# S5 parameter preparation: order of the buffer's memset, the rows, C's turn and the loads of B and C

## The chip, the cores and the metric

The kernel runs on one core of a Trainium2 chip. The metric is the device time of one execution in microseconds (us). The engines are TensorE (PE; its weight loads are PEld), VectorE (DVE), ScalarE (ACT), GpSimd (POOL) and SyncE (SP). SP and POOL issue the DMA transfers that matter here; each engine takes its instructions strictly in program order.

## What is computed

Two layers on a sequence of 256 tokens of 1024 channels, float32. Each layer is FFN, mixer, FFN; mixer 0 is an S5 state-space mixer, mixer 1 a gated MLP.

```
h = LN(alpha*h + 0.5*swiglu(h, w_in[i,0], w_out[i,0]))
h = LN(alpha*h + mixer(h))          # S5 in layer 0, gMLP in layer 1
h = LN(alpha*h + 0.5*swiglu(h, w_in[i,1], w_out[i,1]))
```

The S5 mixer needs parameters that are worked out from its inputs alone:

```
dt = exp(log_dt);  mag = exp(a_re*dt)
lam = mag * (cos(a_im*dt) + i*sin(a_im*dt))
coef = (lam - 1) / (a_re + i*a_im)
bbar = coef * b                     # 64 groups x 64 states x 16 channels
h_t = lam*h_(t-1) + bbar*u_t;  y = Re(c*h)
```

## The kernel before, in words

The order of the instructions is written out by hand. `Stream` (line 44) carries all weights: a block of 128x2048 is loaded by SP into one of 3 raw buffers, split into hi (a cast on ScalarE, line 88) and lo (a subtraction on VectorE, line 89), both in one of 5 split buffers, and used by three matmuls per product (lines 201 to 203 and 208 to 210). `Stream.tick` (line 130) is called after each group of matmuls: it finishes the pending lo's, issues loads, splits a block and then runs one background function. In the first FFN a chunk of 256 hidden columns has four ticks in `chunk_in` (line 373) and two in `step_out`; `start_in` (line 409) is the special first chunk, with three ticks, 0 to 2.

The background of the first FFN is the S5 parameter work of `prepare_s5` (line 620). It is a list of items (first tick, cost, function), lines 941 to 990. Its own `tick` (line 994) adds 1.5 to a credit at each tick, at most to 2.25, and runs items from the head of the list as long as the tick number has reached the item's first tick and the credit is positive or the item's cost is 0:

```
credit[0] = min(credit[0] + PREP_US, 1.5 * PREP_US)
while work and work[0][0] <= ticks[0] and (credit[0] > 0.0 or work[0][1] == 0):
    _, cost, f = work.pop(0)
    credit[0] -= cost
    f()
```

The items that matter:
- `loads` (line 665) is run at once: POOL loads a_re, a_im, log_dt, d and b_glu as rows. `turn_a` (line 674) turns them on TensorE and copies them out on ScalarE; `ws.early` calls it in `start_in`.
- `exp` (line 693) has three parts on VectorE; the first use gives dt, the second mag. `angle` (line 720) multiplies a by dt, reduces the angle and calls Sin on ScalarE. `lambdas`, `coefs`, `coef`, `lam_power` (lines 732 to 764) are small VectorE operations.
- `seed` (line 775) is eight small POOL operations; `base_table` (line 788) is six of them, `table` (line 806) makes the turn tables on VectorE from the base table, which ScalarE copies.
- `load_b(part)` (line 825) issues 8 POOL loads into bq; `copy_b` (line 834) copies them to other partitions on ScalarE.
- `spread` (line 767): POOL writes the factors out (cf<-fac, line 769) and loads them back in another order (fac<-cf, line 771, four loads).
- `clear_rows` (line 838) clears the rows' buffer s on POOL. `b_rows(j, part)` (line 842) multiplies B with the factors (prod) and adds into s on VectorE; `b_turn` (line 851) turns s into w on VectorE and SP writes it to DRAM (rows<-w).
- `c_load(j)` (line 894) issues 8 POOL loads of C into cz; `c_turn` (line 903) turns cz into cc on VectorE, changes a sign, and puts two `pad` copies (ScalarE) into `behind`, which is run at the next tick. `c_lam` and `b_bar` (lines 910, 890) use cc and b.

The large buffers (tag q: s5a, ch, fac, cz, cc, w, tb, b, cl) share a pool of 6; s, pq and k share one buffer (tag bet).

Of the kernel before, what the change touches and what calls it, by code (L numbers as in the profile page):

```python
# [41 lines left out]
class Stream:  # L42
# [41 lines left out]
    def split(self, pieces=1, eng=None):  # L84
        nc = self.nc
        if self.lazy:
            raw, hi, lo = self.next_block()
            nc.scalar.copy(hi, raw)  # L88
            self.unfinished.append(lambda: nc.vector.tensor_tensor(lo, raw, hi.bitcast(F32), op=ALU.subtract))  # L89
            return  # L90
        eng = eng or [nc.vector]
        raw, hi, lo = self.next_block()
        w = SUB // pieces
        for p in range(pieces):
            s = slice(p * w, (p + 1) * w)
            nc.scalar.copy(hi[:, s], raw[:, s])  # L96
            eng[p % len(eng)].tensor_tensor(lo[:, s], raw[:, s], hi[:, s].bitcast(F32), op=ALU.subtract)  # L97
# [57 lines left out]
def hybrid(ctx: ExitStack, tc: tile.TileContext, a: dict, out: bass.AP, subs=SUBS):  # L155
# [24 lines left out]
    ws = Stream(nc, raw_p, split_p)  # L180

    def transpose_split(src, hi, lo, n, perm=False):


        ps = mm_p.tile([P, 512], F32, tag="mm", name="tps")
        for j in range(n):
            nc.tensor.transpose(ps[:, j * P:(j + 1) * P], src[:, j * P:(j + 1) * P], ident)
        v = ps[:, :n * P].rearrange("p (n t) -> p n t", n=n)
        if perm:
            v = v.rearrange("p n (k t) -> p n t k", t=T)  # L190
            hi, lo = (x.rearrange("p n (t k) -> p n t k", t=T) for x in (hi, lo))
        nc.scalar.copy(hi, v)
        nc.vector.tensor_tensor(lo, v, hi.bitcast(F32), op=ALU.subtract)

    def make_xt(t, perm=False, parts=range(2)):
        for g in parts:
            s = slice(4 * g, 4 * g + 4)
            transpose_split(h[t][:, 512 * g:512 * g + 512], xth[t][:, s], xtl[t][:, s], 4, perm)
# [64 lines left out]
    def in_mm(ids, t, ps, ks):  # L263
        for k in ks:
            wh, wl = ws.get(ids[k // 4])
            s = slice(512 * (k % 4), 512 * (k % 4) + 512)
            mm3(ps, xth[t][:, k], xtl[t][:, k], wh[:, s], wl[:, s], k == 0, k == KD - 1)

    def done(ids):
        for i in ids:  # L270
            ws.done(i)
# [61 lines left out]
    def ffn(ids, li, si, first, last):  # L333
# [20 lines left out]
        def in_act(c, t, ps):  # L354
            sgg = g_p.tile([P, 2, FC], F32, tag="sgg", name="sgg")
            sg, g = sgg[:, 0], sgg[:, 1]
            nc.scalar.activation(sg, ps[:, :FC], AF.Silu)
            nc.vector.tensor_tensor(g, ps[:, FC:], sg, op=ALU.mult)
            pend.append((c, t, g))
# [49 lines left out]
        def start_in():  # L409

            ps = [mm_p.tile([P, 512], F32, tag="mm", name="ips") for _ in range(2)]
            mm = lambda t, k: in_mm(ids["in"][0], t, ps[t], [k])
            make_xt(0, parts=[0])
            split = ws.split_pieces(4)
            split(0)
            make_xt(0, parts=[1])
            mm(0, 0)
            split(1)
            make_xt(1)
            mm(0, 1)  # L420
            for k in range(2):
                mm(1, k)
            for k in range(2, 4):
                split(k)
                for t in range(2):
                    mm(t, k)
            ws.early()
            split = ws.split_pieces(4)
            for k in range(4):
                split(k)  # L430
                for t in range(2):
                    mm(t, 4 + k)
                if k >= 2:
                    ws.tick(0)
            ws.fill()
            ws.tick(2)
            for t in range(2):
                in_act(0, t, ps[t])
            done(ids["in"][0])
# [180 lines left out]
    def prepare_s5(sm, qp, dram):  # L620
# [9 lines left out]
        V, G, A = nc.vector, nc.gpsimd, nc.scalar  # L630
        MUL, ADD, SUB, MAX, MIN = ALU.mult, ALU.add, ALU.subtract, ALU.max, ALU.min
# [4 lines left out]
        twice = lambda x: x.unsqueeze(1).broadcast_to([x.shape[0], 2, *x.shape[1:]])  # L636

        def tt(o, x, y, op, e=V):
            e.tensor_tensor(o, x, y, op=op)  # L639
            return o  # L640

        def ts(o, x, s1, op0, s2=None, op1=None, e=V):
            if op1 is None:
                s2, op1 = 1.0, MUL
            e.tensor_scalar(o, x, s1, s2, op0=op0, op1=op1)
            return o
# [6 lines left out]
        val = {}  # L653
# [39 lines left out]
        def exp(x, name):  # L693

            v, k, r, e = small("ex"), small("ek"), small("er"), both("ee")
            o = val[name] = small(name)

            def reduce():
                ts(v, x(), -170.0, MAX, 170.0, MIN)
                ts(k, v, 1.0 / math.log(2.0), MUL, ROUND, ADD)  # L700
                ts(k, k, -ROUND, ADD)
                stt(r, k, -LN2[0], MUL, v, ADD)
                stt(r, k, -LN2[1], MUL, r, ADD)

            def polynomial():
                ts(o, r, 1.0 / 5040.0, MUL)
                for n in (720.0, 120.0, 24.0, 6.0, 2.0, 1.0):
                    stt(o, o, 1.0 / n, ADD, r, MUL)

            def scale():  # L710
                ts(e[:, 0], k, -126.0, MAX, 127.0, MIN)
                tt(e[:, 1], k, e[:, 0], SUB)
                ts(e, e, 127.0, ADD, ROUND, ADD)
                V.tensor_scalar(e.bitcast(I32), e.bitcast(I32), 23, None, op0=ALU.logical_shift_left)
                stt(o, o, 1.0, ADD, e[:, 0], MUL)
                tt(o, o, e[:, 1], MUL)

            return (1.0, reduce), (1.5, polynomial), (1.2, scale)

        def angle():  # L720
            tt(val["ad"], val["aa"], twice(val["dt"]), MUL)
            th, n = val["ad"][:, 1], small("n")
            ts(n, th, 1.0 / (2.0 * math.pi), MUL, ROUND, ADD)
            ts(n, n, -ROUND, ADD)
            for part in TWO_PI:
                stt(th, n, -part, MUL, th, ADD)
            ts(th, th, 3.1415925, MIN, -3.1415925, MAX)
            z = val["zs"][0]
            A.activation(z[:, 0], th, AF.Sin, scale=0.5)
            A.activation(z[:, 1], th, AF.Sin)  # L730
# [143 lines left out]
        def pad(dst, src):  # L874
            for g in range(2):
                s = slice(64 * g, 64 * g + 64)
                A.copy(dst[s, :, g], src[s])

        behind = []
# [23 lines left out]
        def c_turn():  # L903
            cc = val["cc"] = big("cc", [P, 2, PAIRS, 16])
            V.transpose(cc.rearrange("p j q c -> p (j q c)"), val["cz"].rearrange("p j r c -> p (j r c)"))
            ts(cc[:, 1], cc[:, 1], -1.0, MUL)
            for j in range(2):
                behind.append(lambda j=j: pad(val["c", 0, j], cc[:, j]))

        def c_lam(d, j):  # L910
            if d > 1:
# [26 lines left out]
        def add(first, cost, f, *args):  # L938
            work.append((first, cost, lambda: f(*args)))
# [2 lines left out]
        ws.early = turn_a  # L942
        for cost, f in exp(lambda: val["ldt"], "dt"):
            add(1, cost, f)
        add(2, 1.4, angle)
        for part in range(2):
            add(2, 0, load_b, part)
        for cost, f in exp(lambda: val["ad"][:, 0], "mag"):
            add(3, cost, f)
        for part in range(2, 4):  # L950
            add(3, 0, load_b, part)
        add(4, 2.1, lambdas)
        add(4, 0, seed, 0)
        add(5, 1.4, coefs)
# [2 lines left out]
        add(5, 0, spread)  # L957
        for i in range(1, 7):
            add(5, 0, seed, i)
        add(5, 0, clear_rows)  # L960
        for d in (2, 3):
            add(5, 0.9, lam_power, d)
            for n in (32, 64):
                add(5, 0, copy_b, d - 2, n)
        late = [(base_table, level) for level in range(4)]
        for part in range(4):
            for j in range(2):
                add(10, 1.9, b_rows, j, part)
                if part < 2:
                    add(10, 0, copy_b, part + 2, (32, 64)[j])  # L970
                add(10, 1.3, b_turn, j, part)
                if late:
                    add(10, 0, *late.pop(0))
# [4 lines left out]
        for r in range(4):  # L978
            for level in (4, 5):
                add(20, (1.1, 1.9)[level - 4], table, r, level)  # L980
            if r == 1:
                add(20, 0, c_load, 0)
                add(20, 0, c_load, 1)
                add(20, 0, b_load)
        add(20, 0, pads, 2)
        add(30, 1.3, c_turn)
        for f, *args in [(c_lam, 1, 0), (b_bar, 0), (b_bar, 1), (c_lam, 1, 1)] + [(c_lam, d, j) for d in (2, 3) for j in range(2)]:
            add(30, 2.1, f, *args)
        add(50, 0, k_products, 0)
# [320 lines left out]
```

## Time and profile before

| | |
|---|---|
| median of 3 runs | 1002.95 us (1002.23 to 1005.33) |
| the profiled execution | 1001.06 us, span 999.2 us |
| TensorE busy | 955.0 us (96%) |
| VectorE busy | 648.1 us (65%) |
| ScalarE busy | 427.3 us (43%) |
| GpSimd busy | 158.9 us (16%) |

Matmuls are pipelined and their ends are modelled, so a busy TensorE is not TensorE at its peak. A row of a timeline has start, length, engine, line, operation, output<-input, shape and count; what stands in brackets at its end is the idle time of the engine just before and what ended it. POOL's loads appear there as issues, not as transfers. In a table of windows each engine has its busy time and its number of instructions, and the granted clock of TensorE is a share of 2.4 GHz.

### The profile page before, as it was taken

How to read it: one execution, taken by the hardware profiler on the slowest of the kernel's cores; microseconds unless marked ns; L12 is line 12 of the kernel's file. 1: busy time of each engine (PE TensorE's matmuls, PEld its weight loads, DVE VectorE, ACT ScalarE, POOL GpSimd, SP SyncE). 2: the span in 40 equal slices, each digit the busy share in tenths (PEclk: the TensorE clock that was granted, in tenths of full speed). 3: DMA queues.
4: the chain of work that ended last, by engine and by line, in shares of the span. 5: the costliest groups of instructions: out<-in, count | busy, mean ns of one | idle time of the engine just before them, and what ended most of it. 6: DMA issues, size and time to landing. Idle time of an engine off the chain costs nothing.

```text
span 999.2 us, 16604 instructions
## 1 busy us (share of the span) xinstructions
PE 955.0 (96%) x6988; PEld 866.1 (87%) x6988; DVE 648.1 (65%) x804; ACT 427.3 (43%) x507; POOL 158.9 (16%) x248
## 2 busy tenths in 40 slices
PE   6897999999998999999999999999999999999996
PEld 5896898987887779999998899999979879999995
DVE  4756999866897766454549654454698867363544
ACT  4562346633433344434343453434245355343530
POOL 7259152000565010000002000000011010000001
PEclk9898999999999999999999999999999999999999
DMA  9653897884565358464645867464537556646421
GB/s 251 195 177 127 262 292 232 257 320 172 206 233 176 121 182 269 140 224 156 214 166 167 276 214 240 136 228 152 211 127 264 158 169 222 200 168 212 152 102 42
DMA packets 132202, 195.10 MB, mean 195 GB/s; under 512 B 6992, under 2 KB 103808, under 8 KB 132128
## 3 DMA queue, kind: packets, MB, share of 16 engines
q1 hardware_dynamic: 127280, 182.34, 55.1%
q0 software_dynamic: 4560, 11.19, 3.7%
q8 instruction: 54, 0.88, 0.4%
q10 hardware_dynamic: 288, 0.52, 0.1%
q14 instruction: 20, 0.16, 0.0%
HBM read 184.07 MB, written 9.96 MB: 194 GB/s over the span
## 4 chain that ended last, share of the span: by engine, by line
PE 62%; DVE 19%; POOL 6%; issue 5%; DMA 4%; ACT 3%; SPq 0%; POOLq 0%; DVEq 0%; ACTq 0%
PE ips L210 10%; PE ips L209 10%; PE ips L208 10%; PE acc L201 7%; PE acc L202 7%; PE acc L203 7%; DVE lo L89 4%; DVE lo L97 3%; POOL rot L1081 3%; DVE rot L1087 1%; DVE pq L639 1%; DMA raw<-in_ffn_w_out 1%; PE ips L203 1%; DMA tc<-tb 1%; ACT hi L96 1%
## 5 line engine op out<-in xcount | busy, mean ns | idle before, releaser
L210 PE MATMUL ips<-xt,lo 128*128 128x256 f32 x1184 | 338.5, 286 | 13.2 <-DVE lo L89 10.5
L208 PE MATMUL ips<-xt,hi 128*128 128x256 f32 x1184 | 337.7, 285 | 0.0
L209 PE MATMUL ips<-xt,hi 128*128 128x256 f32 x1184 | 337.2, 285 | 0.0
L89 DVE TENSOR_TENSOR lo<-raw,hi 128x2048 fp32r<-128x2048 f32 x107 | 242.9, 2290 | 11.3 <-ACT hi L88 11.2
L210 PEld LDWEIGHTS ips<-xt,lo 128*128 128x128 f32 x1184 | 229.4, 194 | 14.9 <-DVE lo L89 11.9
L208 PEld LDWEIGHTS ips<-xt,hi 128*128 128x128 f32 x1184 | 229.7, 194 | 1.5
L209 PEld LDWEIGHTS ips<-xt,hi 128*128 128x128 f32 x1184 | 229.4, 194 | 1.4
L88 ACT CAST hi<-raw 128x2048 fp32r<-128x2048 f32 x107 | 204.0, 1909 | 48.1 <-PE acc L203 26.5
L201 PE MATMUL acc<-hi,gt 128*128 128x512 f32 x352 | 138.0, 392 | 1.0 <-ACT gt L406 1.0
L202 PE MATMUL acc<-lo,gt 128*128 128x512 f32 x352 | 137.7, 391 | 1.3 <-DVE lo L89 1.3
L398 DVE TENSOR_TENSOR sgg<-ips,sgg 128x256 f32<-128x256 f32 x74 | 31.1, 421 | 163.5 <-ACT sgg L397 163.3
L203 PE MATMUL acc<-hi,gt 128*128 128x512 f32 x352 | 137.1, 389 | 0.0
L397 ACT ACTIVATE sgg<-ips 128x256 f32<-128x256 f32 x74 | 28.4, 383 | 214.3 <-PE ips L210 214.1
L221 POOL TENSOR_SCALAR rstd<-mv 128x1 f32<-128x1 f32 x14 | 10.4, 741 | 635.6 <-DVE mv L247 611.9
L97 DVE TENSOR_TENSOR lo<-raw,hi 128x2048 fp32r<-128x2048 f32 (+1 forms) x54 | 89.7, 1694 | 22.8 <-ACT hi L96 22.8
L201 PEld LDWEIGHTS acc<-hi,gt 128*128 128x128 f32 x352 | 66.2, 188 | 14.4 <-ACT gt L406 1.8
L202 PEld LDWEIGHTS acc<-lo,gt 128*128 128x128 f32 x352 | 66.3, 188 | 14.1 <-DVE lo L89 1.9
L203 PEld LDWEIGHTS acc<-hi,gt 128*128 128x128 f32 x352 | 66.1, 188 | 14.2 <-DVE gt L407 0.3
L96 ACT CAST hi<-raw 128x2048 fp32r<-128x2048 f32 (+1 forms) x54 | 74.5, 1434 | 3.8 <-DMA raw<-in_ffn_w_in 3.1
L407 DVE TENSOR_TENSOR gt<-sgg,gt 128x256 fp32r<-128x256 f32 x74 | 31.6, 427 | 59.9 <-ACT gt L406 59.9
L406 ACT CAST gt<-sgg 128x256 fp32r<-128x256 f32 x74 | 30.0, 406 | 71.8 <-DVE sgg L398 71.7
L201 PE MATMUL ips<-hi,xt 128*128 128x512 f32 x112 | 45.3, 405 | 4.9 <-ACT hi L106 2.7
(231 smaller groups left out, 1224.9 us busy)
## 6 DMA issues: line engine op xcount, KB each, us to landing
raw<-in_ffn_w_in SPq DMA_DIRECT2D x172, 512.0 KB, 5.6
raw<-in_ffn_w_out SPq DMA_DIRECT2D x44, 1024.0 KB, 5.1
raw<-in_g_w_in SPq DMA_DIRECT2D x8, 1024.0 KB, 5.4
rows<-w SPq DMA_DIRECT2D x8, 512.0 KB, 6.1
raw<-in_s_w_in SPq DMA_DIRECT2D x4, 1024.0 KB, 7.3
raw<-in_s_w_glu SPq DMA_DIRECT2D x4, 1024.0 KB, 5.0
w<-rows SPq DMA_DIRECT2D x8, 512.0 KB, 6.4
tc<-tc SPq DMA_DIRECT2D x8, 512.0 KB, 5.8
```

What stands on the lines that cost most here:

```text
L88: nc.scalar.copy(hi, raw)
L89: self.unfinished.append(lambda: nc.vector.tensor_tensor(lo, raw, hi.bitcast(F32), op=ALU.subtract))
L96: nc.scalar.copy(hi[:, s], raw[:, s])
L97: eng[p % len(eng)].tensor_tensor(lo[:, s], raw[:, s], hi[:, s].bitcast(F32), op=ALU.subtract)
L201: nc.tensor.matmul(ps, xh, wh, start=start, stop=False)
L202: nc.tensor.matmul(ps, xh, wl, start=False, stop=False)
L203: nc.tensor.matmul(ps, xl, wh, start=False, stop=stop)
L208: nc.tensor.matmul(ps, wh, xh, start=start, stop=False)
L209: nc.tensor.matmul(ps, wh, xl, start=False, stop=False)
L210: nc.tensor.matmul(ps, wl, xh, start=False, stop=stop)
L398: nc.vector.tensor_tensor(g, ps[:, 1], sg, op=ALU.mult)
L407: nc.vector.tensor_tensor(x[:, 1], g, x[:, 0].bitcast(F32), op=ALU.subtract)
```

## The change

- `turn_a` is called earlier in `start_in`: after the second `make_xt`, ahead of three groups of three matmuls and two split pieces.
- The multiply of a by dt leaves `angle` (VectorE) and becomes `scaled` on POOL, put out as soon as dt is; `angle` costs 1.2 in the list and comes at tick 3.
- All 32 loads of B, `clear_rows` and all 16 loads of C follow `scaled` in POOL's queue. Before, B's loads had nothing to wait for, `clear_rows` followed the seeds and C's loads came with the tables.
- `c_turn` moves from the first tick 30 to 12, ahead of the rows; its two pad copies become an item of their own (`c_pads`) in its old place.
- The rows' first tick is 13 in place of 10.

```diff
@@ start_in
             make_xt(1)
+            ws.early()
             mm(0, 1)
...
-            ws.early()
             split = ws.split_pieces(4)
@@ prepare_s5
+        def scaled():
+            tt(val["ad"], val["aa"], twice(val["dt"]), MUL, G)
+
         def angle():
-            tt(val["ad"], val["aa"], twice(val["dt"]), MUL)
...
+        def c_pads():
             for j in range(2):
-                behind.append(lambda j=j: pad(val["c", 0, j], cc[:, j]))
+                pad(val["c", 0, j], val["cc"][:, j])
...
-        add(2, 1.4, angle)
-        for part in range(2):
+        add(2, 0, scaled)
+        for part in range(4):
             add(2, 0, load_b, part)
+        add(2, 0, clear_rows)
+        for j in range(2):
+            add(2, 0, c_load, j)
+        add(3, 1.2, angle)
         for cost, f in exp(lambda: val["ad"][:, 0], "mag"):
             add(3, cost, f)
-        for part in range(2, 4):
-            add(3, 0, load_b, part)
...
-        add(5, 0, clear_rows)
...
+        add(12, 1.6, c_turn)
         late = [(base_table, level) for level in range(4)]
         for part in range(4):
             for j in range(2):
-                add(10, 1.9, b_rows, j, part)
+                add(13, 1.9, b_rows, j, part)
...
             if r == 1:
-                add(20, 0, c_load, 0)
-                add(20, 0, c_load, 1)
                 add(20, 0, b_load)
         add(20, 0, pads, 2)
-        add(30, 1.3, c_turn)
+        add(30, 0, c_pads)
```

## Rows read from the trace of the kernel before

**Rows 1.** Busy time by engine in windows of 5 us, 75 to 90 us.

```profile
75.00:80.00 5.00, 3.65 (x18) 2.86 (x16) 0.00 (x0) 0.00 (x0) 3.92 (x16) 1.00 0.00 0
80.00:85.00 5.00, 0.00 (x0) 0.00 (x0) 2.89 (x3) 0.00 (x0) 4.65 (x10) 0.85 0.00 0
85.00:90.00 5.00, 4.34 (x18) 4.05 (x19) 4.99 (x5) 0.00 (x0) 4.84 (x8) 0.50 0.68 188
```

Columns: window and its length, then PE, PEld, DVE, ACT and POOL busy us (instructions), TensorE's granted clock, DMA share, GB/s.

**Rows 2.** The same table, one later window of 5 us and one of 25 us.

```profile
110.00:115.00 5.00, 5.00 (x44) 5.00 (x43) 4.93 (x10) 3.69 (x4) 0.00 (x0) 1.00 0.97 306
125.00:150.00 25.00, 24.93 (x186) 23.77 (x186) 24.72 (x47) 12.45 (x16) 14.86 (x20) 1.00 0.98 291
```

**Rows 3.** Timeline of VectorE, 29 to 195 us.

```profile
29.84 0.19 DVE L639 TENSOR_TENSOR dt<-dt,ee 128x32 f32<-128x32 f32 x1
...
50.43 2.34 DVE L89 TENSOR_TENSOR lo<-raw,hi 128x2048 fp32r<-128x2048 f32 x1
...
63.79 0.29 DVE L639 TENSOR_TENSOR ch<-p,q 128x32 f32<-128x32 f32 x2
69.85 1.39 DVE L639 TENSOR_TENSOR prod<-bq,fac 128x512 f32<-128x512 f32 x2 [5.77 <-DMA fac<-cf]
82.11 0.83 DVE L639 TENSOR_TENSOR s<-prod 128x256 f32<-128x256 f32 x2 [10.87 <-POOL s L840]
82.86 2.35 DVE L89 TENSOR_TENSOR lo<-raw,hi 128x2048 fp32r<-128x2048 f32 x1
...
86.29 2.24 DVE L89 TENSOR_TENSOR lo<-raw,hi 128x2048 fp32r<-128x2048 f32 x1
...
155.91 1.25 DVE L905 STREAM_TRANSPOSE cc<-cz 128x1024 f32<-128x1024 f32 x1
157.19 1.23 DVE L645 TENSOR_SCALAR cc<-cc 128x512 f32<-128x512 f32 x1
...
194.88 0.42 DVE L398 TENSOR_TENSOR sgg<-ips,sgg 128x256 f32<-128x256 f32 x1
```

**Rows 4.** Timeline of GpSimd, 4 to 140 us.

```profile
4.24 2.38 POOL L832 DMA_DIRECT2D bq<-in_s_b_re  x4
...
29.00 1.16 POOL L832 DMA_DIRECT2D bq<-in_s_b_im  x2 [1.22 <-DMA bq<-in_s_b_im]
...
58.75 0.62 POOL L769 DMA_DIRECT2D cf<-fac  x1 [5.50 <-DVE fac L639]
...
64.77 0.31 POOL L639 TENSOR_TENSOR zq<-ch 128x64 f32<-128x64 f32 x1
...
81.12 0.95 POOL L840 MEMSET s<- 128x1024 f32 x1
...
129.77 4.50 POOL L901 DMA_DIRECT2D cz<-in_s_c_re  x8
...
136.16 3.88 POOL L901 DMA_DIRECT2D cz<-in_s_c_im  x7 [1.34 <-DMA cz<-in_s_c_re]
```

**Rows 5.** DMA: GpSimd's queue in 4 to 35 us; landing of bq's loads, of b's.

```profile
q0 software_dynamic: 1150, 0.55, 10.6%
...
DMA to landing us min/median/max: 4.6/6.2/7.0
...
b<-in_s_b_im POOLq DMA_DIRECT2D x1, 256.0 KB, 12.1
```

Columns: packets, MB and share of 16 engines' time; us from issue to landing; in the last row KB and us to landing.

**Rows 6.** Timeline of GpSimd, seed 0: its first operation, its seventh and its last.

```profile
48.56 0.29 POOL L639 TENSOR_TENSOR zq<-ch 128x64 f32<-128x64 f32 x1 [18.40 <-DVE ch L645]
...
50.71 2.14 POOL L645 TENSOR_SCALAR zq<-zq 128x32 f32<-128x32 f32 x1
52.93 0.33 POOL L639 TENSOR_TENSOR ch<-ch,zq 128x64 f32<-128x64 f32 x1
```

**Rows 7.** Timeline of ScalarE: the raw values' first copy, the sine's table load.

```profile
16.95 0.21 ACT L685 COPY ch<-aps 128x64 f32<-128x64 f32 x1 [3.49 <-PE aps L680]
...
26.39 1.28 ACT L729 ACT_TABLE_LOAD   x1
```

## The prediction, made before the change was run

> **What bounds the kernel now.** I read the page's chain of waits first: beside TensorE it names VectorE and GpSimd, the latter in the S5 mixer and in the parameter work of the first FFN. The table of 5 us windows then shows the one place after the start and up to 200 us where TensorE has nothing to do for long. From 75 to 90 us it is busy 3.65, 0.00 and 4.34 of 5 us, so 7.0 us are empty, and the granted clock of the last window is 0.50 (half of 2.4 GHz), which costs about half of its 4.34 us, 2.2 us [rows 1]. VectorE is empty at the same time: 0.00 in 75 to 80. Afterwards it is VectorE that sets the pace: 24.72 of 25 us in 125 to 150, and much the same up to 195 [rows 2].
>
> VectorE's own timeline says why. lam_power's last operation is at 63.79. The first product of b_rows starts at 69.85, 5.77 us late, released by the load of the factors (fac<-cf). Its sums start only at 82.11, 10.87 us late, released by GpSimd's memset of s, the rows' buffer [rows 3]. GpSimd's timeline says why that memset is late: it sits in that queue behind seeds 1 to 6, which run from 64.77 to 81.12 [rows 4]. So VectorE loses 16.6 us to two waits, and two "lo" subtractions for the weights (82.86 and 86.29) queue behind them [rows 3]. That starves TensorE.
>
> From 82.11 to the end of the stretch at 194.88 VectorE has 112.8 us of work with nearly no hole [rows 3]. What the change is worth is therefore when that work starts and how much of it was done before.
>
> **When the moved items run.** The credit of the work list gives the ticks. Before: b_rows(0,0) at tick 11, its sums and b_turn after, with ticks 12 and 13 each starting with a lo (the order of the rows at 82.86 and 86.29). After: dt's last part, the multiply by dt on GpSimd, 32 loads of B, the memset and 16 loads of C are all put out at tick 2; lam_power at 10; c_turn at 12; b_rows(0,0) at 13. From tick 37 on both lists stand alike. So two lo's (2.35 and 2.24 us, 4.5 without their overlap) and c_turn (1.25 and 1.23 us, at 155.91 and 157.19) come ahead of the rows [rows 3].
>
> **The memset first.** It costs 0.95 us on GpSimd wherever it stands [rows 4] and now comes ahead of the seeds. The 10.87 us wait goes. What is late next is the factors: b_rows needs cf written out and loaded back, and those transfers are issued by the same GpSimd queue.
>
> **The loads held.** This is the price. Everything queued behind the multiply by dt on GpSimd waits for dt: 48 loads, then seed 0, then the factors' write and reload, then seeds 1 to 6 and the base table. I add up F, the time at which the first product can start.
> - Start: dt is complete at 30.03 [rows 3]. In 4 to 35 us GpSimd's queue took 10.6% of the DMA engines' time [rows 5]; with B gone from there, the block loads that hold up dt come sooner: 10.6% of the 20 us up to the last of them is about 2 us. So 28.0, and 0.3 for the multiply (the shape of the first operation of [rows 6]): 28.3 (27.0 if all 3.3 us of 31 come back, 30.3 if nothing does).
> - 32 loads of B: from 4.24 to 30.16 they took 0.81 us each, held up by earlier ones' landing (6.2 us median, so about 8 in flight); an issue alone is 0.58 [rows 4, 5]. The new stretch has gaps in the weight traffic, so I take 0.70: 22.4 us (18.6 to 25.9).
> - The memset: 1.0.
> - 16 loads of C: 129.77 to 140.04, 10.3 us; alone 9.0 [rows 4]. I take 10.0.
> - Seed 0: 2.7 us is a sixth of the seeds' 16.35 us, run while VectorE stood still [rows 4]; beside a busy VectorE it took from 48.56 to 53.26, 4.7 us, one of its eight operations lasting 2.14 us while a lo ran from 50.43 [rows 3, 6]. I take the middle, 3.7.
> - From the factors' write to the first product: 58.75 to 69.85, 11.1 us [rows 3, 4].
>
> F = 28.3 + 22.4 + 1.0 + 10.0 + 3.7 + 11.1 = 76.5, between 69.4 and 83.3 with all ends taken together.
>
> On the seed the Trainium skill's page "SBUF — State Buffer", section "Who interferes with whom", has a rule against this change: a VectorE operation with two SBUF inputs shuts out a GpSimd operation that reads SBUF. By that rule seed 0 would always pay the 4.7 us, F be 77.5 and the time 1 us later; the 2.14 us row agrees with it.
>
> **c_turn early.** It waits for C: the last load is issued by 61.7, and lands some 6 us later, by about 67.7 (B's median). With c_turn 2.5 and the next lo 2.2 VectorE reaches b_rows at about 72.5, still before F. Below an F of about 69 the gain ends in any case, since VectorE gets there no sooner (64 + 7 - 2).
>
> **The sum.** From F on VectorE has to do the products (1.4) and the 112.8 us less 2.5 and 4.5: 107.2 us. The stretch ends at F + 107.2 in place of 194.9, so the gain is 87.7 - F = 11.2 us. TensorE can follow: it gets back 7.0 us of idle time and 2.2 of slow clock; it ran on from 63.79, VectorE's last operation before the waits, to 78.65, and two more lo's lie ahead of the new wait, so it need not run dry. The remaining 2 us come out of the start, below, or out of its lower pace after 100.
>
> **What costs nothing.** Raw values turned sooner: four small transposes and five copies of some 0.2 us, about 1 us on ScalarE, which stood idle for 3.49 us there until TensorE had come to them [rows 7]. Three groups of three matmuls stand behind them now and hide them. Uncovered they cost 1 us at the start; the wait that goes can give back at most its 3.49. The start does not enter the sum but through dt. The multiply leaves VectorE for GpSimd, 0.3 us. The sine now stands between two SiLUs: one more table load of 1.28 us [rows 7], beside TensorE's matmuls; uncovered, 1.3 us. C's turn takes one of the rows' output buffers (three left): two turns stand between a buffer's uses, more than the 6 us a write needs; uncovered, about 2 us on VectorE. Seeds and base table now run beside VectorE and end about 114, before the first table at about 122; behind that they would hold ScalarE.
>
> **The rivals.**
> - TensorE is the bound: only its idle time returns, 7.0 us, perhaps the clock's 2.2 [rows 1]: about 995. For it: TensorE too shows 24.93 of 25 us in 125 to 150, and at the pace of 110 to 115, 44 matmuls in 5 us, its 186 there take 21.1 us if all are short, more since some are of double length [rows 2]; it has little to spare. Against: what it lacks beyond the 9.2 us is 2 us only, and the start gives some. Chance 0.20.
> - The wait only changes its name: loads at the slow end and all other ends late, F = 83.3 or more, gain under 3 to 4 us: about 1000. For it: the loads did run at 0.81 each under weight traffic. Chance 0.10.
> - Slower: the loads hold the factors back by more than the memset did. With m per load, F = 44.1 + 48m; no gain at m = 0.91, and 0.3% slower at 0.97. If the loads landed as late as the two big loads of b (12.1 us [rows 5], eighths of 1.5), F = 116 and the time is 1031. Against: no such load took over 7.0 us, 0.88 each [rows 5]. A harsher form of it: GpSimd could issue only while VectorE is idle. The 27.5 us of pure issue would not fit into the 16.6 us of its two waits up to 82 [rows 3], so F would pass 82 + 3.7 + 11.1 = 97 and the time 1012. Eight C issues in 4.50 us at 129.77 [rows 4], while VectorE was 99% busy [rows 2], speak against that. Chance of slower, together 0.08. That harsher form is near what the same page of the Trainium skill calls the trap of VectorE blocking DMA, there for VectorE's two-port modes alone; no row here shows it.
>
> **How the numbers follow.** My forecast has 0.62. The profiled execution took 1001.06 us (span 999.2), 1.9 under the median of 1002.95; 1001.06 - 11.2 = 989.9, and on the median 991.8. The range takes the gain at F = 69.4, 18.3 us, as its fast end, 984.6, and nearly no gain, 1000, as its slow one; it leaves out the slower rival and a part of the one before it. A measurement can tell about 0.3%, 3 us, from no change: faster 0.82 (forecast and TensorE's rival), same 0.10, slower 0.08.
>
> **What would show it.** Right: the memset of s before 60 us; no VectorE wait for it; GpSimd issuing loads from about 28 to 62; cf written at about 65; the first product released by fac<-cf at 70 to 83; TensorE without an empty window near 80 and at full clock; the last c_lam about 11 us sooner; the S5 mixer and all behind it as long as before. Wrong: cf written after 75, a VectorE hole of over 15 us ahead of the first product, or ScalarE waiting for the base table near 120.

## The result, and the profile after

The changed kernel took 990.93 us (median of 4 runs, 990.91 to 992.64) against 1003.04 us for the kernel before (median of 4); the ratio is 0.9888, with a 95% interval of 0.9875 to 0.9901. The forecast was 991.8. The profiled execution has a span of 988.9 us, 10.3 less than before.

The same table of 5 us windows as [rows 1], now for the changed kernel:

```profile
75.00:80.00 5.00, 5.00 (x44) 5.00 (x43) 4.29 (x7) 0.45 (x2) 4.09 (x13) 1.00 0.01 3
80.00:85.00 5.00, 5.00 (x43) 4.95 (x42) 4.93 (x10) 4.95 (x5) 4.27 (x12) 1.00 0.38 145
85.00:90.00 5.00, 1.86 (x8) 1.37 (x7) 5.00 (x5) 3.57 (x4) 4.66 (x5) 0.97 0.29 77
90.00:95.00 5.00, 5.00 (x17) 3.90 (x17) 5.00 (x5) 0.00 (x0) 4.59 (x7) 0.69 0.83 292
```

The empty stretch of TensorE around 80 us has gone, and VectorE is busy from 75 us on. A smaller hole of 3.1 us has come up in 85 to 90 us, and the granted clock of the next window is 0.69.

VectorE's timeline after, to be held against [rows 3]:

```profile
26.16 0.19 DVE L639 TENSOR_TENSOR dt<-dt,ee 128x32 f32<-128x32 f32 x1
...
59.52 4.58 DVE L89 TENSOR_TENSOR lo<-raw,hi 128x2048 fp32r<-128x2048 f32 x2
64.40 1.25 DVE L907 STREAM_TRANSPOSE cc<-cz 128x1024 f32<-128x1024 f32 x1 [0.30 <-issue]
65.68 0.43 DVE L645 TENSOR_SCALAR cc<-cc 128x512 f32<-128x512 f32 x1
66.02 2.41 DVE L89 TENSOR_TENSOR lo<-raw,hi 128x2048 fp32r<-128x2048 f32 x1
75.57 1.39 DVE L639 TENSOR_TENSOR prod<-bq,fac 128x512 f32<-128x512 f32 x2 [7.14 <-DMA fac<-cf]
77.07 0.86 DVE L639 TENSOR_TENSOR s<-prod 128x256 f32<-128x256 f32 x2
...
85.98 4.63 DVE L89 TENSOR_TENSOR lo<-raw,hi 128x2048 fp32r<-128x2048 f32 x2
...
117.59 2.26 DVE L639 TENSOR_TENSOR prod<-bq,fac 128x512 f32<-128x512 f32 x2
...
184.07 0.42 DVE L398 TENSOR_TENSOR sgg<-ips,sgg 128x256 f32<-128x256 f32 x1
```

One wait of 7.14 us is left of the two that made 16.6 us, and it is the one for the factors. C's turn and two more lo's than before stand ahead of the rows. The last row is the operation that marked the end of the stretch before, at 194.88; it now comes at 184.07, 10.8 us sooner.

GpSimd's timeline after, to be held against [rows 4]:

```profile
26.51 0.33 POOL L639 TENSOR_TENSOR ch<-ch,dt 128x64 f32<-128x64 f32 x1 [22.25 <-DVE dt L639]
27.02 2.42 POOL L834 DMA_DIRECT2D bq<-in_s_b_re  x4 [0.18 <-issue]
...
39.06 2.31 POOL L834 DMA_DIRECT2D bq<-in_s_b_im  x4
...
44.34 1.16 POOL L834 DMA_DIRECT2D bq<-in_s_b_re  x2 [1.57 <-DMA bq<-in_s_b_re]
...
47.79 0.97 POOL L842 MEMSET s<- 128x1024 f32 x1
48.69 1.68 POOL L903 DMA_DIRECT2D cz<-in_s_c_re  x3
52.02 2.78 POOL L903 DMA_DIRECT2D cz<-in_s_c_re  x5 [1.66 <-DMA bq<-in_s_b_re]
...
58.45 0.56 POOL L903 DMA_DIRECT2D cz<-in_s_c_im  x1 [0.98 <-DMA cz<-in_s_c_re]
59.51 1.74 POOL L903 DMA_DIRECT2D cz<-in_s_c_im  x3 [0.49 <-DMA cz<-in_s_c_re]
61.26 0.70 POOL L639 TENSOR_TENSOR zq<-ch 128x64 f32<-128x64 f32 x1
62.03 2.18 POOL L639 TENSOR_TENSOR ch<-zq 128x32 f32<-128x32 f32 x1
...
66.34 0.62 POOL L771 DMA_DIRECT2D cf<-fac  x1
71.73 2.19 POOL L773 DMA_DIRECT2D fac<-cf  x4 [4.77 <-DMA cf<-fac]
```

The memset stands at 47.79 and nobody waits for it. From 26.51 to 66.34 the queue has nothing but the multiply, 32 loads, the memset, 16 loads and seed 0; its only pauses, 5.8 us in all, are waits for earlier loads to land. The factors, complete on VectorE at about 54.8, are written out at 66.34 only: this is the price of the held loads.

### The profile page after: what moved, and what is told of

Same layout as the page of the kernel before. It is cut to its first block, busy times and chain, and to the rows that moved or that the text cites. A ratio compares the mean times of both kernels' runs of the same rounds, so it can differ in the third digit from the quotient of the medians.

```text
span 988.9 us, 16599 instructions
## 1 busy us (share of the span) xinstructions
PE 950.5 (96%) x6988; PEld 860.9 (87%) x6988; DVE 649.5 (66%) x803; ACT 426.1 (43%) x506; POOL 170.3 (17%) x249
## 3 DMA queue, kind: packets, MB, share of 16 engines
HBM read 184.07 MB, written 9.96 MB: 196 GB/s over the span
## 4 chain that ended last, share of the span: by engine, by line
PE 62%; DVE 18%; DMA 7%; POOL 6%; issue 4%; ACT 3%; SPq 0%; POOLq 0%; DVEq 0%; ACTq 0%
PE ips L210 10%; PE ips L209 10%; PE ips L208 10%; PE acc L201 7%; PE acc L202 7%; PE acc L203 7%; DVE lo L97 3%; DVE lo L89 3%; POOL rot L1085 3%; DMA bq<-in_s_b_re 2%; DVE rot L1091 1%; DVE pq L639 1%; DVE prod L639 1%; DMA raw<-in_ffn_w_out 1%; PE ips L203 1%
## 5 line engine op out<-in xcount | busy, mean ns | idle before, releaser
L210 PEld LDWEIGHTS ips<-xt,lo 128*128 128x128 f32 x1184 | 227.1, 192 | 2.7 <-DVE lo L89 2.7
L208 PEld LDWEIGHTS ips<-xt,hi 128*128 128x128 f32 x1184 | 227.1, 192 | 1.5
L209 PEld LDWEIGHTS ips<-xt,hi 128*128 128x128 f32 x1184 | 227.1, 192 | 1.4
```

The costliest lines, as they stand in the source:

```text
L208: nc.tensor.matmul(ps, wh, xh, start=start, stop=False)
L209: nc.tensor.matmul(ps, wh, xl, start=False, stop=False)
L210: nc.tensor.matmul(ps, wl, xh, start=False, stop=stop)
```

## The experiments

In each, F is the start of the first product on VectorE and E the start of the operation that marks the end of the stretch (194.88 before). The path law of the prediction says E = F + 107.2 when C's turn and two lo's come before F, and E = start of the first sums + 112.8 when none of that does. Ratios are against runs of the kernel before on the same chip.

**The memset alone**, put ahead of the seeds in the kernel before (e1_memset_only):

```diff
+        add(2, 0, clear_rows)
         add(2, 1.4, angle)
...
-        add(5, 0, clear_rows)
```

> The kernel before with one part of the change alone: the memset of the rows' buffer put out at tick 2, ahead of the seeds; loads, C's turn, raw values and rows' tick as before. Theory (VectorE's path law): the sums of the first row start right behind the products, at about 71.2 us in place of 82.1; VectorE's stretch ends about 10.9 us earlier, less 1 us since seeds and base table now run beside a busy VectorE: about 993 us, as fast as the whole change within 2 to 3 us. Rival (the parts add up, and the memset alone returns only TensorE's 7.0 idle us or less): about 996 us or slower. TensorE has no empty 5 us window in either.

Measured: 992.78 us, ratio 0.9910 (0.9891 to 0.9929). VectorE's timeline of this kernel:

```profile
69.99 1.31 DVE L639 TENSOR_TENSOR prod<-bq,fac 128x512 f32<-128x512 f32 x2 [5.14 <-DMA fac<-cf]
71.41 0.86 DVE L639 TENSOR_TENSOR s<-prod 128x256 f32<-128x256 f32 x2
...
186.84 0.41 DVE L398 TENSOR_TENSOR sgg<-ips,sgg 128x256 f32<-128x256 f32 x1
```

The sums follow the products at once. By the law E would be 71.41 + 112.8 = 184.2; it is 186.84, 2.6 us over the law and 8.0 us sooner than before. The moved line alone gives four fifths of what the whole change gives, and the intervals of the two overlap. The rival's gain of 7.0 us or less lies just outside the interval: measured were 8.8 us, 7.1 to 10.9.

**The memset put back** behind the seeds in the changed kernel (e2_memset_back):

```diff
-        add(2, 0, clear_rows)
...
             add(5, 0, seed, i)
+        add(5, 0, clear_rows)
```

> The changed kernel with the memset put back behind seeds 1 to 6. Theory: the first products start at about 75 us as now, the sums wait for the seeds, which then run beside an idle VectorE in some 16 us, so the sums start at about 90 in place of 77: 13 us later, and the time is about 1004 us, as slow as the kernel before. Rival (what counts is the rows' later place and C's early turn): under 995 us.

Measured: 1002.63 us, ratio 1.0009 (0.9998 to 1.0021): the whole gain is gone. Its VectorE timeline:

```profile
77.01 1.39 DVE L639 TENSOR_TENSOR prod<-bq,fac 128x512 f32<-128x512 f32 x2 [8.95 <-DMA fac<-cf]
90.65 0.83 DVE L639 TENSOR_TENSOR s<-prod 128x256 f32<-128x256 f32 x2 [12.25 <-POOL s L842]
...
196.25 0.42 DVE L398 TENSOR_TENSOR sgg<-ips,sgg 128x256 f32<-128x256 f32 x1
```

The wait for the memset is back, 12.25 us. The law with C's turn and two lo's done is 90.65 + 105.8 = 196.4; 196.25 was measured. Here the seeds ran while VectorE stood still, and the law is met to 0.2 us.

**The loads free** (e3_loads_free): the multiply on VectorE again, so that nothing on GpSimd waits for dt.

```diff
-            tt(val["ad"], val["aa"], twice(val["dt"]), MUL, G)
+            tt(val["ad"], val["aa"], twice(val["dt"]), MUL)
```

> The changed kernel with the multiply by dt on VectorE again, so that no load of B or C waits for dt; all else as changed. Theory (the held loads cost): B's loads are issued from 4 to 31 us, C's by 45, cf is written as soon as the factors are there, about 58, so VectorE's wait of 7.1 us for fac<-cf goes; VectorE reaches the first product at about 70 in place of 75.6 and the time falls by 3 to 6 us, to 985 to 988. Rival 1 (TensorE is the bound by then, it was empty for 3 us only after 85): a gain of 0 to 3 us. Rival 2 (holding the loads frees the start's transfers): block loads at the start come 2 to 3 us later, dt at 29 to 30, and the two cancel: 990 to 992.

Measured: 982.33 us, ratio 0.9808 (0.9791 to 0.9824). It beats both kernels, and by more than the theory said. VectorE's timeline and the later windows:

```profile
30.97 0.19 DVE L639 TENSOR_TENSOR dt<-dt,ee 128x32 f32<-128x32 f32 x1
...
69.81 1.50 DVE L639 TENSOR_TENSOR prod<-bq,fac 128x512 f32<-128x512 f32 x2
71.42 0.85 DVE L639 TENSOR_TENSOR s<-prod 128x256 f32<-128x256 f32 x2
...
178.02 0.41 DVE L398 TENSOR_TENSOR sgg<-ips,sgg 128x256 f32<-128x256 f32 x1
```

```profile
80.00:85.00 5.00, 5.00 (x44) 5.00 (x43) 5.00 (x4) 2.95 (x3) 4.75 (x4) 1.00 0.18 50
85.00:90.00 5.00, 5.00 (x36) 4.63 (x35) 4.97 (x5) 0.00 (x0) 4.50 (x8) 1.00 0.89 306
```

No wait stands before the first product, and TensorE has no hole. dt is complete at 31.2, 4.8 us later than in the changed kernel: holding the loads does speed up the start, as rival 2 said. (Of the 4.8 us, 1.7 are one VectorE operation that took 1.88 us in place of 0.20; in the second run of this code it took 0.20 and dt was complete at 29.3.) But F is 5.8 us sooner and E 6.1 us sooner. Run again beside the last kernel of this section (e3_again), the same code gave this:

> The kernel with all loads free once more, beside the one with C alone free, on the same chip: 981 to 984 us, 8 us below the changed kernel; the first products at about 70 us with no wait for the factors.

Measured: 981.46 us, ratio 0.9788 (0.9773 to 0.9803). F is 67.42 and E 175.88.

With the loads free VectorE's end does not set the time any more. The page's chain of work that ended last, in shares of the span, first for the changed kernel and then for this one:

```profile
PE 62%; DVE 18%; DMA 7%; POOL 6%; issue 4%; ACT 3%; SPq 0%; POOLq 0%; DVEq 0%; ACTq 0%
PE 80%; DVE 9%; POOL 4%; ACT 2%; issue 2%; DMA 2%; SPq 0%; POOLq 0%; DVEq 0%; ACTq 0%
```

In the traces of both runs of this code the chain from 50 to 205 us is TensorE's alone, and TensorE is busy throughout; in the changed kernel most of the chain from 75.57 to 184.07 is VectorE's, and TensorE is empty for 5.3 us between 60 and 210. So here the bound has passed to TensorE.

**The raw values turned late** (e4_turn_late): `ws.early()` back at its old place in the changed kernel.

```diff
-            ws.early()
             mm(0, 1)
...
+            ws.early()
             split = ws.split_pieces(4)
```

> The changed kernel with the raw values turned at their old place. Theory: the four split casts wait again for TensorE, dt comes 1 to 2 us later, and so do the loads, F and the end: 992 to 993 us. Rival (the start is bound by the block loads from HBM, so the place of the turn does not matter): 990.5 to 991.5.

Measured: 992.19 us, ratio 0.9905 (0.9884 to 0.9927); the interval holds the changed kernel's ratio, so the time tells nothing. In its trace dt is complete at 29.86 in place of 26.35, F is 77.26 in place of 75.57 and E 185.78 in place of 184.07. F and E are later by 1.7 us, as the theory had it, and that is shown by one trace alone; dt is later by 3.5 us, more than the theory's 1 to 2. The difference was made up on GpSimd: B's loads took 2.1 us longer, but C's 1.7 us less, and seed 0, beside an idle VectorE, 2.6 us in place of 5.0.

**The rows early** (e5_rows_early): rows at first tick 10, C's turn at 30, all else as changed.

```diff
-        add(12, 1.6, c_turn)
...
-                add(13, 1.9, b_rows, j, part)
+                add(10, 1.9, b_rows, j, part)
...
+        add(30, 1.6, c_turn)
         add(30, 0, c_pads)
```

> The changed kernel with the rows back at first tick 10 and C's turn back at 30; loads held, memset first, raw values early as changed. Theory (VectorE's law): the first products still start when the factors land, at about 75.6 us, but two lo's and C's turn, 7.0 us together, are still to be done then, so VectorE's stretch ends 7 us later, at about 191 in place of 184, and the time is 996 to 999 us; TensorE, with two blocks fewer split, stands empty for 5 us or more between 75 and 90. Rival (the order of VectorE's work does not matter since its sum is the same): within 1 us of the changed kernel, about 991.

Measured: 993.85 us, ratio 0.9923 (0.9897 to 0.9949); the interval overlaps the changed kernel's. VectorE's first product and E:

```profile
71.46 1.35 DVE L639 TENSOR_TENSOR prod<-bq,fac 128x512 f32<-128x512 f32 x2 [10.15 <-DMA fac<-cf]
...
187.07 0.42 DVE L398 TENSOR_TENSOR sgg<-ips,sgg 128x256 f32<-128x256 f32 x1
```

Less than expected, because F moved too, by 4.1 us: seed 0 ran beside a VectorE that was idle from 61.3 on and took 3.1 us in place of 5.0, cf was written at 63.91, and the way from there to the first product took 7.6 us in place of 9.2. The law without C's turn and lo's ahead is 71.46 + 1.4 + 112.8 = 185.7; E is 187.07. TensorE is empty for 1.9 us in 75 to 80 at a clock of 0.66. So the later rows and the early turn of C are worth 3.0 us of E here, not 7.0.

**C's loads from SyncE** (e6_c_sync), at tick 6:

```diff
-                    G.dma_start(out=val["cz"][r:r + 16, j], in_=src[sq // 2, sq % 2, e])
+                    nc.sync.dma_start(out=val["cz"][r:r + 16, j], in_=src[sq // 2, sq % 2, e])
...
-            add(2, 0, c_load, j)
...
+            add(4, 0, c_load, j)
         add(4, 2.1, lambdas)
```

> The changed kernel with the 16 loads of C issued by SyncE at tick 6 in place of GpSimd; B's loads still held behind the multiply by dt. Theory: GpSimd's queue is free at about 48 us, seed 0 ends by 53, cf is written as soon as the factors are there at about 55, they land at 65 to 67, and VectorE does not wait for them; the start stays as fast as in the changed kernel (dt complete at 26.4 us and not 31.2 as with all loads free). So it keeps both gains: 979 to 982 us, at or below the 982.3 of the kernel with the loads free. Rival 1 (TensorE is the bound there: it was full in every window from 50 to 200 us with the loads free): 982 to 984. Rival 2 (the 16 issues on SyncE hold up block loads): 985 or more.

Measured: 988.47 us, ratio 0.9863 (0.9837 to 0.9890): the theory's time was missed, and rival 2 is what happened. SyncE's queue and ScalarE's timeline:

```profile
41.55 6.39 SPq L903 DMA_DIRECT2D cz<-in_s_c_re  x8
48.14 4.12 SPq L903 DMA_DIRECT2D cz<-in_s_c_im  x8
52.38 0.39 SPq L63 DMA_DIRECT2D raw<-in_ffn_w_out  x1
```

```profile
58.35 1.90 ACT L88 CAST hi<-raw 128x2048 fp32r<-128x2048 f32 x1 [7.14 <-DMA raw<-in_ffn_w_out]
```

GpSimd's part went as planned: cf was written at 55.31. But a weight block stood behind C's 16 issues on SyncE from 41.55 to 52.38 (the changed kernel issued it at 44.76), ScalarE waited 7.14 us for it, and VectorE stood idle for 8.33 us behind that, against 2.70 in the changed kernel. F was 73.80 and E 182.55. The interval overlaps the changed kernel's, and this trace is of the slowest of the six runs (991.07).

**C loaded twice** (e7_c_twice), the first time into a buffer that nobody reads:

```diff
-        for j in range(2):
-            add(2, 0, c_load, j)
+        for nm in ("cy", "cz"):
+            for j in range(2):
+                add(2, 0, c_load, j, nm)
```

> The changed kernel with C loaded twice by GpSimd, the first time into a buffer that nobody reads: 16 more loads in the queue ahead of the factors. Theory: they cost 9 to 13 us, F moves from 75.6 to 85 to 88, and by gain = 87.7 - F (less the 1.3 us that the law was short by) the kernel is as slow as before, 0 to 2 us of gain: 999 to 1003 us against 1001.6 to 1003. This is the threshold of the slower rival. Rival (the queue on GpSimd is hidden, TensorE or VectorE have other work): 991 to 994.

Measured: 1000.80 us, ratio 0.9988 (0.9971 to 1.0005).

```profile
84.81 1.47 DVE L639 TENSOR_TENSOR prod<-bq,fac 128x512 f32<-128x512 f32 x2 [5.97 <-DMA fac<-cf]
...
193.26 0.42 DVE L398 TENSOR_TENSOR sgg<-ips,sgg 128x256 f32<-128x256 f32 x1
```

The 16 more issues took 12.3 us of GpSimd's queue (48.23 to 60.49) and moved F by 9.2 us; seed 0, beside an idle VectorE, gave 2.4 us back. Nearly all of the gain was eaten. The queue is on the path.

**C first, B held** (e8_c_first):

```diff
+        for j in range(2):
+            add(2, 0, c_load, j)
         add(2, 0, scaled)
...
         add(2, 0, clear_rows)
-        for j in range(2):
-            add(2, 0, c_load, j)
```

> The changed kernel with C's 16 loads ahead of the multiply by dt on GpSimd, so that they go out at the start, and B's 32 loads held behind it. Theory: C takes GpSimd from 4 to 15 us, dt is complete at 27 to 29, B's loads end at 48 to 51, cf is written by 56, the factors land before VectorE has reached the rows at about 68; its stretch then ends at 68 + 107.2 and 1.3, at 176.5 to 178, and the time is 0 to 2 us below that of the kernel with all loads free: 980 to 983 us. Rival (half of the held loads still cost half of what all cost): 986 or more.

Measured: 985.86 us, ratio 0.9832 (0.9816 to 0.9848), against 0.9788 for all loads free on the same chip. F is 68.69 and E 176.89, as expected, but the time is 3 us over and next to the rival's 986. dt was complete at 29.5, no sooner than with all loads free beside it (29.3), so by these two traces 16 loads at the start cost as much there as 48. E is 1.0 us later than with all free; the profiled execution took 983.97, the fastest of its five. Part of the rest lies behind E: the second-next chunk's operation that stands at 211.68 before follows E here after 17.1 us, with all loads free after 15.3. There ScalarE's cast waits for the weight block (w_out) that SyncE issued at 177.00: it starts at 189.87, 12.9 us after the issue, against 11.1 with all loads free. Why the block came later is not shown.

## Why the prediction was right

By its own steps, with F first:

| step | forecast | changed kernel |
|---|---|---|
| multiply by dt ended | 28.3 | 26.84 |
| 32 loads of B | 22.4 | 20.8 (27.02 to 47.80) |
| memset | 1.0 | 0.9 |
| 16 loads of C | 10.0 (9.0 to 10.3) | 12.6 (48.69 to 61.25) |
| seed 0 | 3.7 (2.7 to 4.7) | 5.0 (61.26 to 66.29) |
| cf's write to the first product | 11.1 | 9.2 (66.34 to 75.57) |
| F | 76.5 | 75.57 |
| F to E | 107.2 | 108.5 |
| gain at E | 11.2 | 10.8 |

The mechanism held: the memset's wait was the bound, the held loads put the factors in its place, and VectorE's work from F on set the end. The mechanism was not luck, but that F came out within 0.9 us is: five of the six terms were off by 1.3 to 2.6 us and cancelled. The start, B's loads and the factors' way came out 1.5, 1.6 and 1.9 us shorter, C's loads and seed 0 2.6 and 1.3 us longer. C's 16 loads were outside their bounds, because they waited for B's loads still under way (1.66 us at 52.02) as well as for each other. Seed 0 was beyond its upper end, and the multiply ended before the earliest time allowed for it (27.0).

**The law.** E - F was measured where C's turn and two lo's came first: 108.5 (changed), 108.2 and 108.5 (e3 and e3_again), 108.5 (e4 and e7), 108.8 (e6), 108.2 (e8), against 107.2. The 1.0 to 1.6 us over it are missing in e2, where the seeds did not run beside VectorE. So they lie in GpSimd's work beside VectorE's, which the forecast took as free for VectorE. The products show it: all sixteen took 10.8 us in the kernel before and in e2, and 12.1 to 12.4 us in these seven runs. The longest pair is the row at 117.59: two products took 2.26 us there, 1.39 at 75.57. In e1, 2.6 us over the law's other form, the products took 11.9 us and C's sign change 0.65 us more than before; the rest was not traced.

**The start.** I put 2 us on freeing the first transfers and gave the early turn no part in it. dt came 3.7 us sooner (26.35 for 30.03). Neither part does that alone: with the turn late and the loads held 29.86, with the turn early and the loads free 31.2 and 29.3; the five kernels that have both (changed, e2, e5, e6, e7) lie at 26.0 to 26.7. Both are needed, since ScalarE's casts waited either for the turn (4.27 us in e4) or for the blocks (3.64 us in e3).

**TensorE "need not run dry"** was wrong. It stood empty for 3.1 us in 85 to 90: VectorE came from its wait with the row work of ticks 13 to 15 in hand, and between the lo at 66.02 and the next at 85.98 there was none for 17.6 us. Up to E it cost nearly nothing, as VectorE set the end: e3 has no such hole and its E - F is at most 0.3 us shorter.

**"What costs nothing."** One more table load for the sine was forecast; there is one fewer. Before, ScalarE loaded tables at 26.39 and 32.02; in the changed kernel it did so once, at 22.82, and the sine ran at 28.39 without a load of its own. The base table ended at 119.3 in place of 114, still before the first table's copy at 123.15, so it held up nothing.

**The rivals.** That TensorE is the bound falls for the changed kernel: its time lies 4 us below the rival's 995, its chain is mostly VectorE's from F to E, and with the loads free it gained another 0.8 to 1.0%. But the rival was near: between 60 and 210 us TensorE still stood empty for 5.3 us and lost, by estimate, 1.6 us to the slow clock (0.69 over 90 to 95). With the loads free both are gone, and there TensorE is the bound. The wait under a new name was near: with 16 more loads it happened (e7), at F = 84.81, where the law gives a gain of 2.9 us and 0.12% was measured. (For F = 83.3 the prediction put 3 to 4 us; its own 87.7 - F gives 4.4.) The slower rival's threshold of 0.91 us per load was not reached: the 48 loads took 33.4 us, 0.70 each. Its harsher form, that GpSimd issues only while VectorE is idle, falls as well: four issues took 2.31 us at 39.06, 0.58 each, while a lo ran from 38.64 to 40.92. What the prediction did not ask is whether the loads had to be held at all. e3 says that this part of the change costs 8 to 10 us.

**GpSimd beside VectorE.** In seed 0 the operation at 62.03 took 2.18 us while two lo's ran from 59.52 to 64.10; alone it takes about 0.25. The Trainium skill's page "SBUF — State Buffer", section "Who interferes with whom", says that the one that starts second waits until the other has ended. The trace agrees in both directions: 2.18 us on GpSimd, and the products' 2.26 us on VectorE beside GpSimd operations from 117.35 to 119.30. Seed 0 as a whole took 5.0 us beside the lo's, nearer to the 4.7 of that rule than to the 3.7 taken, and 2.6 us in e4 and e7, where VectorE stood idle.

## What to carry to other kernels

A short operation on a little-used engine can be the bound when it stands behind a long chain in that engine's queue: look at what a waiting row's releaser stood behind, and move that one instruction first. Before a transfer is held behind a value, count everything that is queued after it on the same engine; here 33 us of issues were put ahead of the one write that the next stage needed, and letting them go gave as much again as the fix. The end of a stretch with one busy engine can be forecast from when its backlog starts and what was done before: F + 107.2 was short by only 1.0 to 1.6 us in six kernels. And the bound moves on: once GpSimd's wait was gone VectorE set the end, and with the loads free TensorE did, so what is left to gain has to be read from the new chain and not from the old wait.

## What the runs showed of the hardware that was not expected

C's sign change (128x512, one input) took 1.23 us at 157.19 in the kernel before, where GpSimd began two memsets at 157.20, and 0.43 us in the changed kernel at 65.68, where GpSimd ran only small operations of seed 0 beside it. In e1 and e5 it took 1.88 and 1.26 us, again beside memsets that were running or began with it, and in all three runs it ended 0.3 us after a memset did; in the other runs it took 0.43 to 0.52 us. No run took the memsets alone away, so that they are the cause is argued, not shown.

B's loads landed after 6.2 us (median) in the start's traffic and after 4.4 us in the new stretch, and the queue's pace went from 0.81 to 0.65 us per load, near the 0.58 of an issue alone. In the new stretch the issue itself, not the landing, is most of the cost: 18.6 of 20.8 us for B, 9.0 of 12.6 us for C.
